# Weight casts moved into the first block's loads, and transfers to disjoint parts no longer ordered, in a hybrid decoder layer

## The chip, the cores and the metric

One Trainium2 chip, all 8 cores. Each core runs the same program on one element of the batch. The metric is the device time of the slowest core in microseconds (us), as a median over runs. Some executions of the kernels here fell into a slower state (the cores of a die at a lower mean clock, and a time 2 to 15% longer).

## The reference, cut to what matters

```python
# x: (8, 4096, 1024) float32, one sequence per core
z = h @ w_in                         # -> q | k | v | ssm_u | gates
y_attn = dilated attention, 3 groups of 4 heads, mixed by their softmax denominators
y_ssm  = GLU(gelu(s5_ssm(u)))        # 32 groups of 16 channels, 64 complex states each
mix = (sig(g_s) * (y_ssm @ w_ssm_proj) + sig(g_a) * (y_attn @ w_attn_proj)) @ w_out
h = layer_norm(ALPHA * h + mix)
ff = square(relu(h @ w_up)) @ w_down # 1024 -> 4096 -> 1024
h = layer_norm(ALPHA * h + ff)
```

## The kernel before

The program is written as operations with declared reads and writes of *resources*. A list scheduler fixes the order on each engine ahead of time; semaphores enforce what the resources imply. A transfer must wait, on the queue that issues it, for the last writer of every resource it writes to have *landed*:

```python
for w in writes:
    if w.w is not None and (dma or w.w.dma or w.w.eng != eng or eng != "pe"):
        dep(w.w)                       # write after write, whatever part was written
    ...
```

The stages: U projection and preparation of the SSM matrices; then six attention rounds (two head pairs by three dilations) beside 32 SSM groups, called the mixer stage here; then eight channel blocks of 512 tokens (gates, output projection, up, down). The parts the change touches:

```python
# preparation, per batch of two groups: three stores into disjoint parts, one resource
sres = [sw_res.res[g0 + j] for j in range(GB)]
dma("sp", dst[:, :, 0:640], st.ap, [st], sres)
dma("sp", dst[64:128, :, 640:896], st.ap[0:64, :, 384:640], [st], sres)
dma("sp", dst[0:64, :, 640:896], st.ap[64:128, :, 384:640], [st], sres)
# Toeplitz part: one buffer used twice
for off in range(2):
    for t in range(8): ...             # matmuls, then a copy into mst
    dma("sp", sw_d[:, :, 896 + off*128 : 1024 + off*128]..., mst.ap..., [mst], [mw_res])
# SSM group: two halves in, two halves out
for hf in range(2):
    dma("sp", ug.ap[:, hf, :], ..., [u_res.res[ft]], [ug])
for t in range(2):
    dma("act", y_d[g, :, t*8 : t*8+8]..., ysg.ap[:, t, :], [ysg], [y_res.res[g]])
# weights to bf16: 50 half pieces, memory to memory, paced by the projection's copies
wcast.append(lambda pace, c=c_: dma("pool", dst[i, c], src[i, c]..., pace, [...]))
for name in ("glu", "gate", "sp", "ap", "out", "up", "dn"): ...
# channel blocks: a ring of eight 8 KB slots, filled from the bf16 copies
dma("sp", slot.ap[:, 0:sz], dst[i], res.res[2*i : 2*i+2], [slot])
```

The softmax here doesn't subtract the row's maximum and nothing guards it: scores larger than these inputs give would overflow.

Of the kernel before, what the change touches and what calls it, by code (L numbers as in the profile page):

```python
# [362 lines left out]
def build_program():  # L363
# [33 lines left out]
    tabs_d = dram_tmp("tab_scratch", [32, 128, 2, 256], F32)  # L397
    sw_d = dram_tmp("sw_scratch", [32, 128, 1152], BF16)
    wb = {}
# [4 lines left out]
    u_res = Buf(None, 4)  # L404
    y_res = Buf(None, 32)
    ya_res = Buf(None, 16)
    tabs_res = Buf(None, 16)
    sw_res = Buf(None, 32)
    mw_res = Buf(None, 1)
# [248 lines left out]
    bigAs, bigBs = [f4(), f4()], [f4(), f4()]  # L658
    stg = [ar.alloc([GB, 640], BF16) for _ in range(3)]
    ar.seek(T2, c32.span[0])  # L660
    WSfs = [f4(), f4()]
    stg += [ar.alloc([GB, 640], BF16) for _ in range(2)]
    obi = 0
# [19 lines left out]
    for gb in range(NBATCH):  # L683
        g0 = gb * GB
        st, WSf = stg[gb % len(stg)], WSfs[gb % 2]
        (wA, wB), (lA, lB) = outer_pair(gb)
        tt("dve", WSf.ap, wA.ap, wB.ap, ALU.subtract, [wA, wB], [WSf])
        tt("dve", st.ap[:, :, 384:640], lA.ap.rearrange(flat), lB.ap.rearrange(flat), ALU.subtract, [lA, lB], [st])
        bk = banks[6 + gb % 2]
        for g in range(GB):  # L690
            for hf in range(2):
                lhs = WSf.ap[:, g, hf * 8:hf * 8 + 8, :].rearrange("p s h -> p (s h)")
                tr(bk.ap[:, (g * 2 + hf) * 128:(g * 2 + hf + 1) * 128], lhs, ident_f, [WSf, smP], [bk])
                mm(cols[hf].ap[:, (g0 + g) * 16:(g0 + g + 1) * 16], lhs, c1.ap[:, g0 + g, :], True, True,
                   [WSf, c1], [cols[hf]])
        wx = st.ap[:, :, 0:384].rearrange("p g (f q) -> p g f q", f=2)
        src = bk.ap.rearrange("p (g f q) -> p g f q", g=GB, f=2)
        cp("act", wx[:, :, :, 0:128], src, [bk], [st])
        cp("act", wx[:, :, :, 128:192], src[:, :, :, 0:64], [bk], [st])
        sres = [sw_res.res[g0 + j] for j in range(GB)]  # L700
        dst = sw_d[g0:g0 + GB].rearrange("g p q -> p g q")
        dma("sp", dst[:, :, 0:640], st.ap, [st], sres)
        dma("sp", dst[64:128, :, 640:896], st.ap[0:64, :, 384:640], [st], sres)
        dma("sp", dst[0:64, :, 640:896], st.ap[64:128, :, 384:640], [st], sres)
    ar.seek(argm.span[0], Xb.span[0])
    colb = [ar.alloc([512], BF16) for _ in range(2)]
    ar.seek(Q1u, A0)
    mst = ar.alloc([32, 8, 16], BF16)
    cp("act", colb[0].ap, cols[0].ap, [cols[0]], [colb[0]])
    tt("dve", colb[1].ap, cols[1].ap, sb_("ddiag"), ALU.add, [cols[1], smB], [colb[1]])  # L710
    n = 0
    for off in range(2):
        for t in range(8):
            bk = banks[4 + n % 4]
            n += 1
            d = 128 + 16 * (7 - t)
            mm(bk.ap, shf.ap[:, d:d + 128], colb[1 - off].ap, True, off == 0, [shf, colb[1 - off]], [bk])
            if off:
                d = 128 - 16 * (t + 1)
                mm(bk.ap, shf.ap[:, d:d + 128], colb[1].ap, False, True, [shf, colb[1]], [bk])  # L720
            cp("act" if t % 2 else "dve", mst.ap[:, :, t, :], bk.ap.rearrange("p (g h) -> p g h", h=16), [bk], [mst])
        dma("sp", sw_d[:, :, 896 + off * 128:1024 + off * 128].rearrange("g p q -> p g q"),
            mst.ap.rearrange("p g t h -> p g (t h)"), [mst], [mw_res])

# [37 lines left out]
    tabb = [ar.alloc([2, 256], F32) for _ in range(NS)]  # L762
    swb = [ar.alloc([1152], BF16) for _ in range(NS)]
    ugb = [ar.alloc([2, 256], BF16) for _ in range(NS)]
    t12 = ar.alloc([2, 256], F32)
# [6 lines left out]
    def ssm_in(g):  # L772
        tb, sw, ug = tabb[g % NS], swb[g % NS], ugb[g % NS]
        ft, h0 = g // 8, (g % 8) * 16
        for hf in range(2):
            dma("sp", ug.ap[:, hf, :], u_d[ft, h0:h0 + 16, hf * 8:hf * 8 + 8].rearrange("h s c -> s h c"),
                [u_res.res[ft]], [ug])
        dma("sp", sw.ap, sw_d[g], [sw_res.res[g], mw_res], [sw])
        dma("sp", tb.ap, tabs_d[g], [tabs_res.res[g // 2]], [tb])

    def ssm_z(g):
        sw, ug, bk = swb[g % NS], ugb[g % NS], banks[6]
        for z in range(2):
            for hf in range(2):
                o = hf * 192 + z * 64
                mm(bk.ap[:, z * 256:(z + 1) * 256], sw.ap[:, o:o + 128], ug.ap[:, hf, :], hf == 0, hf == 1,
                   [sw, ug], [bk], skip_group_check=True)

# [9 lines left out]
    def ssm_y(g):  # L798
# [11 lines left out]
        for t in range(2):  # L810
            dma("act", y_d[g, :, t * 8:t * 8 + 8].rearrange("h t c -> t h c"), ysg.ap[:, t, :], [ysg], [y_res.res[g]])

# [30 lines left out]

    for name in ("glu", "gate", "sp", "ap", "out", "up", "dn"):
        for i in range(len(wb[name][2].res) // 2):
# [169 lines left out]
    y2T = ar.alloc([4, 512], BF16, nres=4)  # L1015
    yab = ar.alloc([2, 512], BF16)
    sg = ar.alloc([512], F32)
    gsb, gab = ar.alloc([512], F32), ar.alloc([512], F32)
    ar.seek(E0, S1)
    yf = ar.alloc([4, 512], F32)  # L1020
    mixin = ar.alloc([8, 512], BF16, nres=8)
# [30 lines left out]
    def last_use(slot):  # L1052
        rs = slot.res[0]
        return max([o.seq for o in rs.r.values()] + [rs.w.seq if rs.w is not None else 0])

    def load_piece(name, i):
        slot = min((r for r in ring if id(r) not in live), key=last_use)
        live.add(id(slot))
        dst, _, res, sz = wb[name]
        dma("sp", slot.ap[:, 0:sz], dst[i], res.res[2 * i:2 * i + 2], [slot])  # L1060
        return slot
# [27 lines left out]
    def load_g(blk):  # L1089
        P.at("p3l", 6)  # L1090
        dma("pool", xTb.ap, xB_d[blk], [], [xTb])
        for kc in range(4):
            src = y_d[kc * 8:(kc + 1) * 8].rearrange("g h t c -> (g h) t c")[:, 2 * blk:2 * blk + 2, :]
            dma("sp", yf.ap[:, kc, :].rearrange("p (t c) -> p t c", t=2), src, [y_res.res[kc * 8 + j] for j in range(8)], [yf])
        act(yT.ap, yf.ap, AF.Gelu_apprx_tanh, [yf], [yT])
        for p4 in range(2):
            dma("sp", yab.ap[:, p4, :].rearrange("p (r c) -> p r c", r=2), ya_d[p4, :, 2 * blk:2 * blk + 2, :],
                [ya_res.res[p4 * 8 + blk]], [yab])

# [72 lines left out]
    def stage_up(blk):  # L1172
        P.at("p3", 7)
        for up in range(8):
            piece = load_piece("up", up)
            for m4 in range(4):
# [31 lines left out]
    for blk in range(NB):  # L1208
# [6 lines left out]
        P.at("p3", 7)  # L1215
        pcs = [load_piece("dn", q) for q in range(4)]
        if nxt:
            wo = [load_piece("out", oh) for oh in range(2)]
        pcs2 = [load_piece("dn", 4 + q) for q in range(2)]
        for t in range(TB):  # L1220
# [5 lines left out]
        if nxt:  # L1226
            done(*wo)
        pcs2 += [load_piece("dn", 6 + q) for q in range(2)]
        for t in range(TB):
# [73 lines left out]
```

## Time and profile before

| | before |
|---|---|
| median of 4 runs | 2152.30 us (2149.72 to 2153.1) |
| profiled run, slowest core | 2179.7 us |
| first load of the GLU weights, mean of the 8 cores | 694 us |
| from there to the last output store of block 1, mean of the 8 cores | 470.7 us |

The first GLU load ("first glu load") can only be issued when the last projection has read the input, so it marks how long the token mixers take. The second span (its end is the eighth store of the output) covers channel blocks 0 and 1, and so the place to which the change moves the casts. The lines of this profile stand in the prediction.

### The profile page before, as it was taken

Reading aid. Unit: us, or ns where it says so; the run is one execution under the profiler, and the core shown is the slowest. Engines: PE = TensorE matmul, PEld = TensorE weight load, DVE = VectorE, ACT = ScalarE, POOL = GpSimd, SP = SyncE. Lnnn points to the kernel's source line nnn. Section 1 sums busy time; section 2 is a strip of 40 time slices with the busy share of each in tenths; the row PEclk is TensorE's granted clock in tenths of the full one; section 3 lists DMA queues with packets and bytes.
Section 4 is the critical chain, followed back from the end, with each engine's and each line's share of the span. In section 5 each row is a group of like instructions: output and inputs, shape, how many; then the busy total and the mean of one; then the engine's idle time right before and its main releaser. Section 6 shows DMA issues by size and latency. Waiting matters only on the chain.

```text
span 2179.7 us, 31231 instructions; the slowest of 8 cores (2140.6 to 2179.7 us)
## 1 busy us (share of the span) xinstructions
PE 1929.6 (89%) x10468; PEld 943.1 (43%) x10468; DVE 952.5 (44%) x1396; ACT 696.2 (32%) x1053; POOL 300.2 (14%) x338
## 2 busy tenths in 40 slices
PE   3898278866879769999999999999999999999996
PEld 1455144634445334444444444444444444444443
DVE  6641255523432443364255355355345436424523
ACT  2553244533335623313312422421421421321120
POOL 6651012211210200100100100010010010010000
PEclk8999589978889889999999999999999999988898
DMA  9867567876763754456466466357447445533430
GB/s 167 175 197 113 117 156 155 151 140 145 153 133 128 233 168 152 150 172 243 140 192 241 136 188 251 136 158 276 142 144 250 181 140 186 216 107 136 176 116 39
DMA packets 112380, 359.71 MB, mean 165 GB/s; under 512 B 18240, under 2 KB 55488, under 8 KB 85184
## 3 DMA queue, kind: packets, MB, share of 16 engines
q1 hardware_dynamic: 79344, 265.33, 35.9%
q0 software_dynamic: 24176, 83.99, 19.5%
q10 hardware_dynamic: 8704, 8.39, 1.2%
q8 instruction: 88, 1.44, 0.3%
q14 instruction: 68, 0.56, 0.1%
HBM read 356.72 MB, written 74.97 MB: 198 GB/s over the span
## 4 chain that ended last, share of the span: by engine, by line
PE 66%; DMA 16%; DVE 6%; ACT 5%; issue 4%; ACTq 1%; SPq 1%; POOL 1%; DVEq 0%; POOLq 0%
PE ps L450 65%; DMA sw_scratch<-arena 6%; DMA y_scratch<-arena 5%; DVE arena L490 4%; ACT arena L496 2%; DMA arena<-u_scratch 2%; ACT arena L462 2%; DVE arena L480 1%; PE ps L455 1%; ACTq L440 1%; SPq L440 1%; ACT L462 1%; DMA arena<-x_tile 1%; DVE arena L1075 1%; DMA tab_scratch<-arena 0%
## 5 line engine op out<-in xcount | busy, mean ns | idle before, releaser
L450 PE MATMUL ps<-arena 128*128 128x512 bf16 (+3 forms) x10148 | 1912.1, 352 | 194.7 <-ACT arena L496 62.6
L450 PEld LDWEIGHTS ps<-arena 128*128 128x128 bf16 (+1 forms) x10148 | 926.8, 105 | 1162.2 <-issue 408.7
L462 ACT ACTIVATE arena<-ps 128x512 f32<-128x512 f32 (+2 forms) x384 | 261.0, 680 | 434.6 <-PE ps L450 340.8
L480 DVE TENSOR_TENSOR arena<-arena 128x512 f32<-128x512 f32 (+7 forms) x267 | 187.5, 725 | 232.2 <-ACT arena L462 165.3
L490 DVE SCALAR_TENSOR_TENSOR arena<-ps,arena 128x512 bf16<-128x512 f32 x256 | 176.9, 691 | 253.1 <-ACT arena L462 253.1
L480 POOL TENSOR_TENSOR arena<-arena 128x512 bf16<-128x512 f32 (+1 forms) x128 | 161.8, 1267 | 802.7 <-DVE arena L480 696.0
L480 DVE TENSOR_TENSOR arena<-ps,arena 128x512 f32<-128x512 f32 (+1 forms) x193 | 127.6, 688 | 328.7 <-PE ps L450 269.6
L462 ACT ACTIVATE arena<-arena 128x512 f32<-128x512 f32 (+6 forms) x186 | 101.3, 547 | 319.1 <-DVE arena L1077 262.0
L496 ACT CAST arena<-ps 128x512 bf16<-128x512 f32 (+1 forms) x217 | 120.8, 569 | 215.5 <-PE ps L450 138.4
L490 DVE SCALAR_TENSOR_TENSOR arena<-arena,ps 128x512 f32<-128x512 f32 x128 | 87.1, 686 | 216.6 <-PE ps L450 215.1
L490 DVE SCALAR_TENSOR_TENSOR arena<-arena 128x1024 f32<-128x1024 f32 (+1 forms) x131 | 167.1, 1276 | 21.7 <-ACT arena L462 6.6
L462 ACT ACTIVATE arena<-ps,arena 128x512 f32<-128x512 f32 x128 | 86.0, 686 | 177.7 <-POOL arena L480 140.7
L440 POOL DMA_DIRECT2D out<-arena x32 | 17.3, 542 | 646.6 <-DVE arena L490 646.6
L1075 DVE BATCH_NORM_STATS2 arena<-arena 128x6 f32<-128x512 f32 x128 | 88.8, 694 | 12.9 <-DVE arena L1075 0.5
L462 ACT ACT_TABLE_LOAD x42 | 53.9, 1283 | 121.0 <-DVE arena L1077 106.0
L496 ACT COPY arena<-ps 128x512 f32<-128x512 f32 (+1 forms) x64 | 51.1, 799 | 97.7 <-DMA y_scratch<-arena 56.8
L455 PE MATMUL ps<-arena 128*128 128x128 bf16 (+1 forms) x320 | 40.9, 248 | 38.8 <-ACT arena L496 22.2
L496 ACT CAST arena<-arena 128x1024 bf16<-128x1024 f32 x32 | 33.4, 1045 | 104.3 <-DVE arena L490 104.3
L455 PEld LDWEIGHTS ps<-arena 128*128 128x128 bf16 (+1 forms) x320 | 30.5, 126 | 57.3 <-issue 56.6
L480 DVE TENSOR_TENSOR arena<-arena,ps 128x512 f32<-128x512 f32 x64 | 41.0, 682 | 6.5 <-PE ps L450 6.3
L486 POOL TENSOR_SCALAR arena<-arena 128x256 f32<-128x256 f32 x32 | 39.9, 1248 | 15.6 <-DMA tab_scratch<-arena 13.0
L497 DVE CAST arena<-ps 128x512 bf16<-128x512 f32 x8 | 5.5, 692 | 71.0 <-DMA sw_scratch<-arena 61.0
(28 smaller groups left out, 166.2 us busy)
## 6 DMA issues: line engine op xcount, KB each, us to landing
arena<-wb_up SPq DMA_DIRECT2D x64, 1024.0 KB, 10.6
arena<-wb_dn SPq DMA_DIRECT2D x64, 1024.0 KB, 5.9
arena<-wb_gate SPq DMA_DIRECT2D x32, 1024.0 KB, 5.9
arena<-wb_out SPq DMA_DIRECT2D x16, 1024.0 KB, 4.9
arena<-x POOLq DMA_DIRECT2D x32, 512.0 KB, 9.2
out<-arena POOLq DMA_DIRECT2D x32, 512.0 KB, 4.0
arena<-sw_scratch SPq DMA_DIRECT2D x32, 288.0 KB, 7.1
arena<-x_tile POOLq DMA_DIRECT2D x8, 1024.0 KB, 49.4
```

The lines of the kernel that those rows point to most:

```text
L440: return P.add(eng, lambda e: e.dma_start(out=out, in_=in_), R(*reads), R(*writes), dma=True, nbytes=nb)
L450: return P.add("pe", lambda e: e.matmul(out, lhsT, rhs, start=start, stop=stop, **kw), R(*reads), R(*writes), cost=c)
L455: return P.add("pe", lambda e: e.transpose(out, in_, ident), R(*reads), R(*writes), cost=c)
L462: return P.add("act", lambda e: e.activation(out, in_, func, bias=bias, scale=scale), R(*reads), R(*writes), cost=c, aset=ASETS.get(func))
L480: return P.add(eng, lambda e: e.tensor_tensor(out, in0, in1, op), R(*reads), R(*writes), cost=ew_cost(eng, out, [in0, in1], True))
L486: return P.add(eng, lambda e: e.tensor_scalar(out, in0, s1, None, op0), R(*reads), R(*writes), cost=c)
L490: return P.add("dve", lambda e: e.scalar_tensor_tensor(out, in0, scalar, in1, op0, op1), R(*reads), R(*writes), cost=160.0 + 1.06 * fsize( ...
L496: return P.add("act", lambda e: e.copy(out, in_), R(*reads), R(*writes), cost=c)
L497: return P.add(eng, lambda e: e.tensor_copy(out, in_), R(*reads), R(*writes), cost=c)
L1075: P.add("dve", (lambda hf_: lambda e: e.bn_stats(st6[:, hf_ * 6:hf_ * 6 + 6], xb.ap[:, hf_ * 512:hf_ * 512 + 512]))(hf), R(xb), R(m), cost ...
```

## The change

The intent is twofold. Transfers that write disjoint parts get a resource each, so that none waits for a sibling to land; the two stores of the Toeplitz matrix become one with long rows. And the up and down weights are no longer cast from memory to memory during the mixer stage: the loads of the first channel block cast them into the ring, and the slot is stored from there for the other seven blocks. The diff, cut to its core:

```diff
-    y_res = Buf(None, 32)
+    y_res = Buf(None, 64)
-    sw_res = Buf(None, 32)
+    sw_res = Buf(None, 96)
...
-        dma("sp", dst[:, :, 0:640], st.ap, [st], sres)
-        dma("sp", dst[64:128, :, 640:896], st.ap[0:64, :, 384:640], [st], sres)
-        dma("sp", dst[0:64, :, 640:896], st.ap[64:128, :, 384:640], [st], sres)
+        dma("sp", dst[64:128, :, 640:896], st.ap[0:64, :, 384:640], [st.res[1]], sres[1])
+        dma("sp", dst[0:64, :, 640:896], st.ap[64:128, :, 384:640], [st.res[1]], sres[2])
+        dma("sp", dst[:, :, 0:640], st.ap, [st], sres[0])
...
-    ar.seek(Q1u, A0)
-    mst = ar.alloc([32, 8, 16], BF16)
+    ar.seek(Q1, A0)
+    mst = ar.alloc([32, 2, 8, 16], BF16, nres=16)
...
-        dma("sp", sw_d[:, :, 896 + off * 128:1024 + off * 128].rearrange("g p q -> p g q"),
-            mst.ap.rearrange("p g t h -> p g (t h)"), [mst], [mw_res])
+    dma("sp", mw_d, mst.ap.rearrange("p g o t h -> p g (o t h)"), [mst], [mw_res])
...
-                [u_res.res[ft]], [ug])
-        dma("sp", sw.ap, sw_d[g], [sw_res.res[g], mw_res], [sw])
+                [u_res.res[ft]], [ug.res[hf]])
+        dma("sp", sw.ap[:, 0:896], sw_d[g], sw_res.res[3 * g:3 * g + 3], [sw.res[0]])
+        dma("sp", sw.ap[:, 896:1152], mw_d[:, g, :], [mw_res], [sw.res[1]])
...
-            dma("act", y_d[...], ysg.ap[:, t, :], [ysg], [y_res.res[g]])
+            dma("act", y_d[...], ysg.ap[:, t, :], [ysg], [y_res.res[g * 2 + t]])
...
-    for name in ("glu", "gate", "sp", "ap", "out", "up", "dn"):
+    for name in ("glu", "gate", "sp", "ap", "out"):
...
+        if first:
+            was = P.stream, P.prio
+            P.at("p3c", 5)
+            dma("pool", slot.ap[:, 0:sz], src[i].rearrange("p k c -> p (k c)"), [], [slot])
+            dma("sp", dst[i], slot.ap[:, 0:sz], [slot], res.res[2 * i:2 * i + 2])
+            P.at(*was)
+        else:
+            dma("sp", slot.ap[:, 0:sz], dst[i], res.res[2 * i:2 * i + 2], [slot])
...
-            piece = load_piece("up", up)
+            piece = load_piece("up", up, blk == 0)
...
-        pcs = [load_piece("dn", q) for q in range(4)]
+        pcs = [load_piece("dn", q, blk == 0) for q in range(4)]
```

The cuts are the new scratch tables, the choice of a ring slot, the same step for the staging buffers, for the gelu input and the attention input of the channel blocks (one resource a part), and the other down loads.

More of the change, by code (lines that the diff above doesn't have):

```diff
@@ L397, in build_program @@
     tabs_d = dram_tmp("tab_scratch", [32, 128, 2, 256], F32)
-    sw_d = dram_tmp("sw_scratch", [32, 128, 1152], BF16)
+    sw_d = dram_tmp("sw_scratch", [32, 128, 896], BF16)
+    mw_d = dram_tmp("mw_scratch", [128, 32, 256], BF16)
     wb = {}
@@ L658, in build_program @@
     bigAs, bigBs = [f4(), f4()], [f4(), f4()]
-    stg = [ar.alloc([GB, 640], BF16) for _ in range(3)]
+    stg = [ar.alloc([GB, 640], BF16, nres=2) for _ in range(3)]
     ar.seek(T2, c32.span[0])
     WSfs = [f4(), f4()]
-    stg += [ar.alloc([GB, 640], BF16) for _ in range(2)]
+    stg += [ar.alloc([GB, 640], BF16, nres=2) for _ in range(2)]
     obi = 0
@@ L687, in build_program @@
         tt("dve", WSf.ap, wA.ap, wB.ap, ALU.subtract, [wA, wB], [WSf])
-        tt("dve", st.ap[:, :, 384:640], lA.ap.rearrange(flat), lB.ap.rearrange(flat), ALU.subtract, [lA, lB], [st])
+        tt("dve", st.ap[:, :, 384:640], lA.ap.rearrange(flat), lB.ap.rearrange(flat), ALU.subtract, [lA, lB], [st.res[1]])
         bk = banks[6 + gb % 2]
@@ L697, in build_program @@
         src = bk.ap.rearrange("p (g f q) -> p g f q", g=GB, f=2)
-        cp("act", wx[:, :, :, 0:128], src, [bk], [st])
-        cp("act", wx[:, :, :, 128:192], src[:, :, :, 0:64], [bk], [st])
-        sres = [sw_res.res[g0 + j] for j in range(GB)]
+        cp("act", wx[:, :, :, 0:128], src, [bk], [st.res[0]])
+        cp("act", wx[:, :, :, 128:192], src[:, :, :, 0:64], [bk], [st.res[0]])
+        sres = [[sw_res.res[(g0 + j) * 3 + part] for j in range(GB)] for part in range(3)]
         dst = sw_d[g0:g0 + GB].rearrange("g p q -> p g q")
-        dma("sp", dst[:, :, 0:640], st.ap, [st], sres)
-        dma("sp", dst[64:128, :, 640:896], st.ap[0:64, :, 384:640], [st], sres)
-        dma("sp", dst[0:64, :, 640:896], st.ap[64:128, :, 384:640], [st], sres)
+        dma("sp", dst[64:128, :, 640:896], st.ap[0:64, :, 384:640], [st.res[1]], sres[1])
+        dma("sp", dst[0:64, :, 640:896], st.ap[64:128, :, 384:640], [st.res[1]], sres[2])
+        dma("sp", dst[:, :, 0:640], st.ap, [st], sres[0])
     ar.seek(argm.span[0], Xb.span[0])
     colb = [ar.alloc([512], BF16) for _ in range(2)]
-    ar.seek(Q1u, A0)
-    mst = ar.alloc([32, 8, 16], BF16)
+    ar.seek(Q1, A0)
+    mst = ar.alloc([32, 2, 8, 16], BF16, nres=16)
     cp("act", colb[0].ap, cols[0].ap, [cols[0]], [colb[0]])
@@ L720, in build_program @@
                 mm(bk.ap, shf.ap[:, d:d + 128], colb[1].ap, False, True, [shf, colb[1]], [bk])
-            cp("act" if t % 2 else "dve", mst.ap[:, :, t, :], bk.ap.rearrange("p (g h) -> p g h", h=16), [bk], [mst])
-        dma("sp", sw_d[:, :, 896 + off * 128:1024 + off * 128].rearrange("g p q -> p g q"),
-            mst.ap.rearrange("p g t h -> p g (t h)"), [mst], [mw_res])
+            cp("act" if t % 2 else "dve", mst.ap[:, :, off, t, :], bk.ap.rearrange("p (g h) -> p g h", h=16), [bk],
+               [mst.res[off * 8 + t]])
+    dma("sp", mw_d, mst.ap.rearrange("p g o t h -> p g (o t h)"), [mst], [mw_res])
     P.at("tabs", 3)
@@ L762, in build_program @@
     tabb = [ar.alloc([2, 256], F32) for _ in range(NS)]
-    swb = [ar.alloc([1152], BF16) for _ in range(NS)]
-    ugb = [ar.alloc([2, 256], BF16) for _ in range(NS)]
+    swb = [ar.alloc([1152], BF16, nres=2) for _ in range(NS)]
+    ugb = [ar.alloc([2, 256], BF16, nres=2) for _ in range(NS)]
     t12 = ar.alloc([2, 256], F32)
@@ L786, in ssm_z @@
                 mm(bk.ap[:, z * 256:(z + 1) * 256], sw.ap[:, o:o + 128], ug.ap[:, hf, :], hf == 0, hf == 1,
-                   [sw, ug], [bk], skip_group_check=True)
+                   [sw.res[0], ug.res[hf]], [bk], skip_group_check=True)
     def ssm_scan(g):
@@ L810, in ssm_y @@
         for t in range(2):
-            dma("act", y_d[g, :, t * 8:t * 8 + 8].rearrange("h t c -> t h c"), ysg.ap[:, t, :], [ysg], [y_res.res[g]])
+            dma("act", y_d[g, :, t * 8:t * 8 + 8].rearrange("h t c -> t h c"), ysg.ap[:, t, :], [ysg], [y_res.res[g * 2 + t]])
     for g in range(NS):
@@ L1015, in build_program @@
     y2T = ar.alloc([4, 512], BF16, nres=4)
-    yab = ar.alloc([2, 512], BF16)
+    yab = ar.alloc([2, 512], BF16, nres=2)
     sg = ar.alloc([512], F32)
@@ L1019, in build_program @@
     ar.seek(E0, S1)
-    yf = ar.alloc([4, 512], F32)
+    yf = ar.alloc([4, 512], F32, nres=4)
     mixin = ar.alloc([8, 512], BF16, nres=8)
@@ L1053, in last_use, with load_piece @@
         rs = slot.res[0]
-        return max([o.seq for o in rs.r.values()] + [rs.w.seq if rs.w is not None else 0])
-    def load_piece(name, i):
+        return max([o.seq for o in list(rs.r.values()) + rs.rd] + [rs.w.seq if rs.w is not None else 0])
+    def load_piece(name, i, first=False):
         slot = min((r for r in ring if id(r) not in live), key=last_use)
         live.add(id(slot))
-        dst, _, res, sz = wb[name]
-        dma("sp", slot.ap[:, 0:sz], dst[i], res.res[2 * i:2 * i + 2], [slot])
+        dst, src, res, sz = wb[name]
+        if first:
[6 more added lines that the diff above has]
+            dma("sp", slot.ap[:, 0:sz], dst[i], res.res[2 * i:2 * i + 2], [slot])
         return slot
@@ L1093, in load_g @@
             src = y_d[kc * 8:(kc + 1) * 8].rearrange("g h t c -> (g h) t c")[:, 2 * blk:2 * blk + 2, :]
-            dma("sp", yf.ap[:, kc, :].rearrange("p (t c) -> p t c", t=2), src, [y_res.res[kc * 8 + j] for j in range(8)], [yf])
+            dma("sp", yf.ap[:, kc, :].rearrange("p (t c) -> p t c", t=2), src,
+                [y_res.res[(kc * 8 + j) * 2 + blk // 4] for j in range(8)], [yf.res[kc]])
         act(yT.ap, yf.ap, AF.Gelu_apprx_tanh, [yf], [yT])
@@ L1097, in load_g @@
             dma("sp", yab.ap[:, p4, :].rearrange("p (r c) -> p r c", r=2), ya_d[p4, :, 2 * blk:2 * blk + 2, :],
-                [ya_res.res[p4 * 8 + blk]], [yab])
+                [ya_res.res[p4 * 8 + blk]], [yab.res[p4]])
     def stage_g(blk):
@@ L1215, in build_program @@
         P.at("p3", 7)
-        pcs = [load_piece("dn", q) for q in range(4)]
+        pcs = [load_piece("dn", q, blk == 0) for q in range(4)]
         if nxt:
             wo = [load_piece("out", oh) for oh in range(2)]
-        pcs2 = [load_piece("dn", 4 + q) for q in range(2)]
+        pcs2 = [load_piece("dn", 4 + q, blk == 0) for q in range(2)]
         for t in range(TB):
@@ L1227, in build_program @@
             done(*wo)
-        pcs2 += [load_piece("dn", 6 + q) for q in range(2)]
+        pcs2 += [load_piece("dn", 6 + q, blk == 0) for q in range(2)]
         for t in range(TB):
```

## The prediction

> **What bounds the kernel now.** I read the page's slices first, then the windows table, the chain, the waits, and the transfer issues; all on the slowest core (span 2179.7 us). The slices show two programs in one: the token mixers (up to about 700 us) with TensorE (PE) full of holes, and the channel-block loop after about 810 us with PE full.
>
> ```profile
> PE   3898278866879769999999999999999999999996
> ...
> PEclk8999589978889889999999999999999999988898
> DMA  9867567876763754456466466357447445533430
> ```
>
> One digit is 54.5 us. From slice 16 on PE is at 9 everywhere. Slice 5 (218 to 272 us) is 2, and its clock is 5. The windows table (busy us, instructions, granted clock, DMA share, GB/s) puts sizes on it:
>
> ```profile
> 150.00:200.00 50.00, 50.00 (x450) 32.46 (x449) 16.46 (x22) 20.89 (x39) 12.49 (x16) 1.00 0.66 115
> 200.00:250.00 50.00, 12.17 (x103) 7.33 (x102) 0.89 (x2) 3.51 (x6) 2.02 (x4) 0.64 0.66 110
> ...
> 400.00:500.00 100.00, 68.04 (x560) 41.18 (x558) 39.44 (x62) 40.77 (x66) 17.47 (x22) 0.86 0.78 149
> 500.00:600.00 100.00, 73.89 (x602) 45.55 (x602) 39.19 (x59) 35.86 (x51) 18.28 (x23) 0.85 0.67 141
> ...
> 1000.00:1100.00 100.00, 100.00 (x465) 45.36 (x464) 35.09 (x54) 34.77 (x50) 11.21 (x10) 1.00 0.51 169
> ```
>
> No engine is busy in 200:250, and in 400:600 none is near full. So the first stage is bound by waits, not by an engine. Which waits, the chain of work that ended last tells, first in shares, then in order of time:
>
> ```profile
> PE ps L450 65%; DMA sw_scratch<-arena 6%; DMA y_scratch<-arena 5%; DVE arena L490 4%; ACT arena L496 2%; DMA arena<-u_scratch 2%; ACT arena L462 2%; DVE arena L480 1%; PE ps L455 1%; ACTq L440 1%; SPq L440 1%; ACT L462 1%; DMA arena<-x_tile 1%; DVE arena L1075 1%; DMA tab_scratch<-arena 0%
> ```
>
> ```profile
> 189.50 5.85 DMA sw_scratch<-arena
> 196.20 31.12 DMA sw_scratch<-arena
> 227.44 2.10 DMA sw_scratch<-arena
> 230.33 2.42 DMA sw_scratch<-arena
> 232.87 2.10 DMA sw_scratch<-arena
> ...
> 488.38 15.12 DMA y_scratch<-arena
> ```
>
> From 66 to 248 us the chain is one store into sw_scratch after another: each batch writes three disjoint parts, but all three carry the same resource, so the sync queue waits for one to land before it issues the next. The later pieces are the second half of each y store waiting for the first, on ScalarE's queue. The waits view says who pays:
>
> ```profile
> DVE arena L497 <- DMA sw_scratch<-arena: 61.0, 1, 61.0
> ACT arena L496 <- DMA y_scratch<-arena: 56.8, 12, 10.0
> PE ps L450 <- DVE arena L497: 38.4, 2, 37.8
> ...
> SPq L222 <- DMA arena<-u_scratch: 183.7, 30, 17.3
> SPq L222 <- DMA sw_scratch<-arena: 98.3, 27, 30.3
> ```
>
> The 61 us wait is the copy of the second half of the Toeplitz matrix (mst), whose buffer is held until the first half's store lands at 248.2. PE stands in that queue for 37.8 us. Attention's first round also needs the memory of the preparation, so its chain starts only at 257 us, and the state-space groups (SSM) at 262.
>
> [...] the shortest pieces above are 2.10 us for 64 KB, and in traffic they are 5 to 8, once 31. [...] clock 0.64 in 200:250, 0.85 in 400:600, 1.00 where PE is dense. A filled hole is thus worth more than its length.
>
> **The change, part by part.**
>
> 1. *Store order in the preparation.* 48 stores of 16 batches wait only for their data; before, 32 of them waited for a sibling to land too. Batches pass PE's f32 transposes at 46, 53, 56, 60, 65, 70 us, some 4.8 us each while the five staging buffers last, then at 78, 94, 111 ... 175: about 10.5 each, because buffers come free with landings. Unblocked, the last batch is due near 46 + 15 x 4.8 = 118 us, say 130 with the tables beside it. The two mst stores of 4096 packets of 256 B become one of 128 rows of 16 KB, and no copy waits for a store. But mst now lies on the U staging buffers, so it waits for the last u store (147.5, landed about 150). Its 24 matmuls and 16 copies took 180 to 188 and 248 to 254, so some 14 us: mst is ready at about 165, SSM starts near 172 to 180 instead of 262.
>
> 2. *What that start is worth on PE.* PE is full from 100 to 212 us anyway (U, first projections), so the 85 us of earlier start are not all gained. PE's busy time before 695 us, where the last projection ends and the first ring loads are issued, is 165 (to 212) + 1 (to 250) + 337 (250 to 695) = 503 us, so 192 us are idle: 47 before 100 us, where the x loads bind (DMA share about 1.0) and nothing changes; 38 in 212 to 250, which goes entirely; 108 in 250 to 695.
>
> 3. *u loads and y stores.* Of the chain, y_scratch is 5.2% (113 us) and u_scratch 1.9% (41 us). These waits disappear: the two halves no longer wait for each other, and ScalarE no longer holds the exponentials of attention behind a landing. In place of these 154 us stands the next limit, the order of work on PE, ScalarE and VectorE. An attention round costs PE about 41 us of projection + 20 of attention + 6 of SSM, and took 60 to 95. I take 60% of the 108 us as recoverable: 65. The clock should rise from 0.86 to about 0.9; of 337 us that is some 10.
>
> 4. *Weight casts leave the mixer stage.* 32 casts of up and down, 512 KB each, are no longer in GpSimd's queue among the SSM products (its waits for wb_up and wb_dn pacing were 86 + 65 + 23 us, mostly idle time that costs nothing) nor on the DMA engines: each cast is 16 packets of 32 KB, which averaged 3660 ns in the trace's transfer records, so 3.7 us of all 16 engines per cast, 117 us in all. I count this inside the 60%.
>
> 5. *They come back in channel block 0.* A piece is now a cast load of 1 MB plus a store of 1 MB, instead of a load of 1 MB. The x_blk load has exactly that form:
>
> ```profile
> arena<-wb_up SPq DMA_DIRECT2D x64, 1024.0 KB, 10.6
> ...
> arena<-x_blk POOLq DMA_DIRECT2D x8, 1024.0 KB, 13.5
> ```
>
> Its packets average 676 ns for 8 KB in the transfer records, 128 x 676 / 16 = 5.4 us of all engines; a plain load or store 128 x 340 / 16 = 2.7 us. So 8.1 instead of 2.7 us per piece, against 6.9 us of PE per piece (32 matmuls of 216 ns). Sixteen pieces add 16 x 5.4 = 86 us of transfers. From 695 to 811 us the DMA share was 0.76 and 0.60 (80 us of 116), from 811 to 984 it was 0.46 (80 of 173). Six up pieces fit in front, during the gates and the serial layer norms; ten come later. The shares then come to (80 + 6 x 5.4) / 116 = 0.97 and (80 + 10 x 5.4) / 173 = 0.77. It fits, but not without stalls: I allow 15 us.
>
> *Sum:* 38 + 65 + 10 - 15 = 98 us on this core. The seven other blocks (172.3 us each) stay. 2152 - 98 x 0.97 (I take a little off, as the timed runs are 1% shorter) gives **2057 us**.
>
> **The rivals.** *(a) Another wait takes over.* With the stores gone, the mixer stage could stay at its 75% PE: the fixed order of instructions, the single score banks and the exponential (1.02 us a unit, 96 units) give a latency chain of their own. For it: in 250 to 475 us, two and a bit rounds took 219 us although the y stores were only part of the chain. Then only the 38 us and about 25 more come back: 2152 - 63 + 15 = 2104. *(b) Block 0 starves.* The weight store sits in the sync queue and waits there for its cast load (13.5 us); glu, gate and down loads behind it wait too. If each of the 16 costs 4 us on PE, that is 64 instead of 15 us lost: 2107. Against it: eight ring slots and the slack of the layer norms. *(c) Fuller recovery.* If attention and SSM become PE-bound, all 108 us of holes go and the clock reaches 0.95: 38 + 108 + 25 - 10 = 161, so 1993. Against it: from 600 to 650 us, when the y stores thin out, PE was busy for 36 of 50 us only. [...] Some cores show clock 0.81 for stretches of 200 us[...].
>
> **Range and chances.** (a) and (b) each near 2105, (c) near 1995; both (a) and (b) at once would give about 2155. So 2020 to 2105. The 2% line is 2109: faster 0.90, within 2% 0.08, slower 0.02.
>
> **What would show it.** Right: the chain after has no run of sw_scratch stores and y_scratch well under 1%; PE above 0.8 in every slice from 2 to 12; the first SSM loads at 165 to 185; the first glu load at 585 to 615 instead of 695; the time from the first to the third glu load, which holds block 0 (696 to 993 us before, 297), 5 to 30 us longer; later blocks at 172. Wrong: the first glu load after 640 (rival a), block 0 more than 40 us longer with PE idle under DMA names (rival b), or a first glu load before 570 (rival c).

## The result, and the profile after

The change takes 2053.36 us (median of 4 runs, of which one, 2177.2 us, is slow), against 2152.3 for the kernel before: a ratio of 0.954 (95% interval 0.952 to 0.956). A ratio is always the mean time of one kernel's fast runs over that of the other's fast runs of the same rounds, so not quite the ratio of the medians. The predicted time was 2057.

The slices of the page (one digit is 51.3 us here) and the chain's shares, slowest core, answer to those of before:

```profile
PE   3898777999977697999999999999999999999996
...
PEclk8999987999988898999999999999999999999998
DMA  9946887551169949974565447366356543633521
...
PE ps L451 72%; DVE arena L491 4%; ACT arena L497 3%; ACT arena L463 2%; DVE arena L481 2%; DMA arena<-wb_out 1%; DMA y_scratch<-arena 1%; ACTq L441 1%; PE ps L456 1%; DMA wb_out<-w_out 1%; DMA arena<-x_tile 1%; ACT L463 1%; DVE arena L1084 1%; DMA tab_scratch<-arena 1%; DMA wb_ap<-w_attn_proj 0%
```

The 2 in PE's slice 5 is gone (the first slice is 1, as in the prediction), sw_scratch is out of the chain, and y_scratch fell from 5% to 1%. But PE is not full from slice 2 on: 7 stands in slices 5 to 7, where the transfer engines are at 8, 8 and 7, and PE dips again in slices 12 to 14 (564 to 718 us, 6 in the last) and 16 (770 to 821 us). The windows of the mixer stage (busy us by engine PE, PEld, DVE, ACT, POOL; then granted clock, DMA share, GB/s):

```profile
200.00:250.00 50.00, 39.98 (x265) 21.48 (x264) 26.00 (x42) 23.10 (x32) 11.71 (x13) 0.95 0.86 179
...
300.00:350.00 50.00, 33.74 (x162) 16.27 (x160) 14.40 (x24) 11.19 (x19) 10.84 (x12) 0.77 0.81 184
...
400.00:500.00 100.00, 95.04 (x805) 56.89 (x804) 51.28 (x76) 53.84 (x81) 16.45 (x15) 1.00 0.42 110
```

Where PE is at 95% the DMA share is 0.42; where it is at 67 to 80% it is above 0.8. The chain in order of time has, among its long pieces:

```profile
254.16 24.57 DMA y_scratch<-arena
...
299.25 9.19 DMA wb_ap<-w_attn_proj
...
318.31 7.75 DMA wb_out<-w_out
...
333.46 11.77 DMA wb_out<-w_out
...
795.27 29.59 DMA arena<-wb_out
```

The first four lie in 254 to 346 us, among the 18 casts that are left (glu, gate, sp, ap, out; issued from 197 to 347 us). The last lies in channel block 0: an output weight load that took 29.6 us to land, among cast loads. In numbers, over the eight cores: the first glu load comes at 568 us instead of 694 (126 us gained), and from there to the end of block 1 it takes 492.6 us instead of 470.7 (21.9 lost). The difference, 104 us, is the 99 of the times but for the difference between profiled and timed runs.

So the predicted total came out, with a larger gain and a larger loss than in its sum (113 and 15). Whether it came out for the stated reasons is another matter, and what the experiments are for.

### The profile page after: what moved, and what is told of

Same layout as the page of the kernel before. It is cut to its first block, busy times and chain, and to the rows that moved or that the text cites.

```text
span 2052.5 us, 31367 instructions; the slowest of 8 cores (2035.6 to 2052.5 us)
## 1 busy us (share of the span) xinstructions
PE 1876.9 (91%) x10468; PEld 924.2 (45%) x10468; DVE 957.9 (47%) x1396; ACT 695.1 (34%) x1053; POOL 295.2 (14%) x322
## 4 chain that ended last, share of the span: by engine, by line
PE 73%; DVE 8%; DMA 6%; issue 6%; ACT 5%; ACTq 1%; POOL 1%; DVEq 0%; POOLq 0%; SPq 0%
PE ps L451 72%; DVE arena L491 4%; ACT arena L497 3%; ACT arena L463 2%; DVE arena L481 2%; DMA arena<-wb_out 1%; DMA y_scratch<-arena 1%; ACTq L441 1%; PE ps L456 1%; DMA wb_out<-w_out 1%; DMA arena<-x_tile 1%; ACT L463 1%; DVE arena L1084 1%; DMA tab_scratch<-arena 1%; DMA wb_ap<-w_attn_proj 0%
## 5 line engine op out<-in xcount | busy, mean ns | idle before, releaser
L451 PE MATMUL ps<-arena 128*128 128x512 bf16 (+4 forms) x10148 | 1859.2, 345 | 118.2 <-DMA arena<-x_tile 27.4
L451 PEld LDWEIGHTS ps<-arena 128*128 128x128 bf16 (+2 forms) x10148 | 909.3, 104 | 1049.1 <-issue 215.0
L481 DVE TENSOR_TENSOR arena<-arena 128x512 f32<-128x512 f32 (+7 forms) x267 | 193.7, 750 | 180.0 <-ACT arena L463 167.1
L1084 DVE BATCH_NORM_STATS2 arena<-arena 128x6 f32<-128x512 f32 x128 | 88.8, 694 | 12.2
L456 PEld LDWEIGHTS ps<-arena 128*128 128x128 bf16 (+1 forms) x320 | 28.9, 121 | 61.7 <-issue 61.5
L488 DVE TENSOR_SCALAR arena<-arena 128x512 f32<-128x512 f32 (+2 forms) x19 | 9.5, 503 | 42.8 <-POOL arena L487 42.4
```

Of the source, the lines that this page charges most:

```text
L451: return P.add("pe", lambda e: e.matmul(out, lhsT, rhs, start=start, stop=stop, **kw), R(*reads), R(*writes), cost=c)
L456: return P.add("pe", lambda e: e.transpose(out, in_, ident), R(*reads), R(*writes), cost=c)
L481: return P.add(eng, lambda e: e.tensor_tensor(out, in0, in1, op), R(*reads), R(*writes), cost=ew_cost(eng, out, [in0, in1], True))
L488: return P.add(eng, lambda e: e.tensor_scalar(out, in0, s1, s2, op0, op1), R(*reads), R(*writes), cost=c)
L1084: P.add("dve", (lambda hf_: lambda e: e.bn_stats(st6[:, hf_ * 6:hf_ * 6 + 6], xb.ap[:, hf_ * 512:hf_ * 512 + 512]))(hf), R(xb), R(m), cost ...
```

## The experiments

Two theories at the start. **Theory 1**, the prediction's: the order of the transfers makes the gain, and the moved casts are a net loss in block 0. **Theory 2**: the casts, while they run beside attention and SSM, are dear, and moving them out is a good part of the gain. Results are summed up here; the column "scaled" is the ratio times 2152 and makes runs on different chips comparable within the intervals (some 4 us either way for the change, up to 29 for uy_back). "Front" is the first glu load and "blocks 0, 1" the span from it to the last output store of block 1, both means over the eight cores of the profiled run.

| kernel | median us | ratio to before (95%) | scaled | front | blocks 0, 1 |
|---|---|---|---|---|---|
| before | 2152.3 | 1 | 2152 | 694 | 470.7 |
| the change | 2053.4 | 0.954 (0.952 to 0.956) | 2053 | 568 | 492.6 |
| order_only | 2106.2 | 0.975 (0.971 to 0.978) | 2097 | 640 | 471.8 |
| weights_only | 2095.9 | 0.968 (0.966 to 0.971) | 2084 | 605 | 492.4 |
| prep_back | 2084.4 | 0.963 (0.960 to 0.966) | 2072 | 596 | 493.2 |
| uy_back | 2093.9 | 0.962 (0.948 to 0.975) | 2070 | 587 | 492.2 |
| order_pad | 2095.3 | 0.972 (0.964 to 0.980) | 2092 | 623 | 472.1 |
| tiny_casts | 2078.3 | 0.953 (0.948 to 0.959) | 2052 | 576 | 493.4 |
| after_pad | 2054.4 | 0.951 (0.948 to 0.955) | 2047 | 569 | 491.9 |
| order_nohold | 2098.0 | 0.972 (0.966 to 0.979) | 2093 | 631 | 477.1 |
| late_store | 2034.8 | 0.942 (0.939 to 0.945) | 2027 | 567 | 475.9 |
| all_first | 2031.9 | 0.940 (0.937 to 0.944) | 2024 | 530 | 512.4 |
| late_r4 | 2005.5 | 0.930 (0.924 to 0.937) | 2002 | 538 | 477.6 |
| ordered_r4 | 2040.7 | 0.946 (0.942 to 0.950) | 2036 | 567 | 480.7 |

A median here is over all runs, slow ones too (uy_back and tiny_casts had two each; the change, weights_only, prep_back and order_pad one each). All twelve gave correct results. The scheduler plans every kernel anew. The lists of PE, VectorE and ScalarE are in the same order in order_only, order_pad, order_nohold and tiny_casts, and in the change and after_pad; every other comparison has a changed order of instructions in it too.

### The two halves apart: order_only and weights_only

order_only is the change with the weight part undone:

```diff
-    for name in ("glu", "gate", "sp", "ap", "out"):
+    for name in ("glu", "gate", "sp", "ap", "out", "up", "dn"):
-            piece = load_piece("up", up, blk == 0)
+            piece = load_piece("up", up)
     # and the same for every load of "dn"
```

> Only the unordered transfers; up and down weights are cast memory to memory in the mixer stage, as before. Theory 1 (the order of transfers makes the gain, the weight move costs block 0 some 27 us and gives little back): first glu load at 570 to 590 us, first to third glu load back near 298 us, time 2025 to 2045. Theory 2 (the weight move frees the mixer stage and is a good part of the gain): first glu load at 630 or later, time over 2085.

weights_only is the kernel before with that part alone:

```diff
-    for name in ("glu", "gate", "sp", "ap", "out", "up", "dn"):
+    for name in ("glu", "gate", "sp", "ap", "out"):
+    load_piece(name, i, first=False)   # as in the change; up and dn with first = (blk == 0)
```

> Only the weight move; all transfers ordered as before. Theory 1: first glu load near 690, first to third glu load 320 to 330, time 2160 to 2180, so slower than before. Theory 2: first glu load near 640, time about 2110 to 2130.

Theory 1 missed on both. Order alone brought 55 us (scaled) where it was to bring 107 to 127, and the weight move alone, which was to make the kernel slower, brought 68. Theory 2 was right on order_only and too small on weights_only (640 us of front and 2110 to 2130 expected, 605 and 2096 measured). Block 0 loses its 21 us in both kernels that move the casts and in neither that does not; but the front gains 89 us by the weight move alone (694 to 605), and 72 with the order already changed (640 to 568). The order is worth 54 us of front without the weight move and 37 with it. So the two share a cause, and the larger part is the weight move.

What the casts do stands in order_only's chain, in order of time:

```profile
298.44 9.86 DMA wb_ap<-w_attn_proj
...
319.04 8.76 DMA wb_out<-w_out
...
411.60 41.31 DMA ya_scratch<-arena
...
471.52 45.10 DMA arena<-bias_t
```

ya_scratch is a store of 128 KB, bias_t a load of 256 KB. In the kernel before, their medians to landing were 5.0 and 8.3 us; here two of them took 41 and 45, and attention stood behind each. The windows of the same kernel show PE and the engines' load:

```profile
400.00:450.00 50.00, 33.11 (x172) 15.86 (x172) 14.25 (x23) 19.43 (x32) 9.93 (x13) 0.88 0.93 147
450.00:500.00 50.00, 37.25 (x385) 26.57 (x385) 17.08 (x25) 14.62 (x25) 10.45 (x14) 0.91 0.86 142
500.00:550.00 50.00, 26.94 (x157) 13.08 (x158) 15.32 (x23) 16.84 (x24) 5.17 (x7) 0.70 0.74 144
```

PE has 27 to 37 of 50 us where the change has 95 of 100. That compares two orders of instructions; tiny_casts, below, keeps the order.

### The order, part by part: prep_back and uy_back

prep_back is the change with the preparation's stores ordered as before (one resource per staging buffer and group, two mst stores through one buffer; an SSM group then loads both parts in one transfer again, which the cut leaves out):

```diff
-        dma("sp", dst[64:128, :, 640:896], ..., [st.res[1]], sres[1])
-        dma("sp", dst[0:64, :, 640:896], ..., [st.res[1]], sres[2])
-        dma("sp", dst[:, :, 0:640], st.ap, [st], sres[0])
+        dma("sp", dst[:, :, 0:640], st.ap, [st], sres)
+        dma("sp", dst[64:128, :, 640:896], ..., [st], sres)
+        dma("sp", dst[0:64, :, 640:896], ..., [st], sres)
```

> The change with the preparation's stores ordered as before (one resource per staging buffer and group, two mst stores through one buffer). Theory 1: the hole after 212 us returns, time 2053 + 38 to 60 = 2091 to 2113. Rival (the SSM and attention stage makes up for a late start, since y stores no longer hold it): no more than 2070.

uy_back is the change with the two halves of a u load and of a y store ordered again:

```diff
-                [u_res.res[ft]], [ug.res[hf]])
+                [u_res.res[ft]], [ug])
-            dma("act", ..., [ysg], [y_res.res[g * 2 + t]])
+            dma("act", ..., [ysg], [y_res.res[g]])
```

> The change with the two halves of each u load and of each y store ordered again. Theory 1: about 65 us of holes return, time 2053 + 50 to 80 = 2103 to 2133. Rival (a landing wait of 5 us per group is hidden by prefetch and by other work): no more than 2075.

Undoing the preparation's part costs 19 us scaled (28 of front, 31 in the medians), less than the 38 to 60 of theory 1 and a little more than its rival allowed. The hole did return (the last Toeplitz store was issued at 252 to 257 us, before at 251 to 262), but part of it was made up later. Undoing u and y costs some 16 (19 of front; the fast runs were 2070, 2077 and 2094, so the interval is wide), not 50 to 80. In that respect the rival was right: with the up and down casts gone, a landing wait per group is mostly hidden. The two parts add up to 47 us of front, against 37 for the whole order (605 to 568), so each is known to about 10 us only.

### What a cast costs beside attention: tiny_casts, order_pad, order_nohold

Three ways in which a cast could hurt: its bytes on the transfer engines; its wait in GpSimd's fixed order, among the SSM products; and its packets, 32 KB each. tiny_casts is the change plus 32 casts of 16 rows of 128 B in the old places, told to the scheduler as full-sized, so that the order of the mixer stage is that of order_only (PE's and ScalarE's lists of instructions are the same but for line numbers):

```diff
+    o = dma("pool", dmy_d[j], src[i, h0:h0 + 16, 0, 0:64], pace, [])
+    o.nbytes = 64 * 4096 * 2           # what the scheduler reckons with
```

> The change, plus 32 tiny cast transfers (16 rows of 128 B) in the places of the up and down casts, with the same waits on GpSimd and the same hold on their pacing buffers; the order of the mixer stage's instructions is that of order_only. Theories A and bytes: first glu load near 565 to 580, time near the change's 2053, at most 2065. Theory of GpSimd's waits or of the order of instructions: first glu load near 646, time 2125 to 2135 (block 0's loss on top).

The front is 576 us against 640 in order_only. So 64 of the 72 us go with the bytes; the waits on GpSimd and the order of instructions account for the other 8 at most (one die of this run had a lower clock, 0.944 against 0.962, and the later fronts; the other die alone has 573, against 638 in order_only). The stretch in which order_only had 27 to 37 of 50 us of PE is full, with the same instructions in the same order:

```profile
400.00:450.00 50.00, 48.65 (x476) 33.15 (x473) 26.18 (x39) 25.96 (x44) 15.23 (x20) 1.00 0.53 141
450.00:500.00 50.00, 49.73 (x430) 29.41 (x429) 24.23 (x38) 28.74 (x40) 10.31 (x16) 1.00 0.32 78
500.00:550.00 50.00, 47.47 (x371) 25.60 (x369) 22.63 (x37) 28.33 (x39) 3.26 (x7) 0.97 0.15 27
```

order_pad is order_only with the rows of the bf16 copies padded, in the same order of instructions:

```diff
-        wb[name] = (dram_tmp("wb_" + name, [n, 128, sz], BF16), ...)
+        wb[name] = (dram_tmp("wb_" + name, [n, 128, sz + 64], BF16)[:, :, 0:sz], ...)
```

> As order_only (same order of instructions on PE, VectorE, ScalarE and the sync queue), but the rows of the bf16 weight copies in memory are padded by 128 B, so that a cast moves 64 packets of 8 KB and not 16 of 32 KB; the bytes stay. Theory A (the 32 KB packets hold each transfer engine for some 4 us, and small transfers queue behind one of them at every packet): first glu load near 570 to 600 instead of 646, time 2050 to 2075, and the 41 and 45 us landings of ya_scratch and bias_t are gone. Theory B (bytes on the engines, or GpSimd's paced waits, are what costs): 2095 to 2110 as before.

The packets became 8 KB as meant, but the front moved only from 640 to 623, and the time by less than the intervals. In the trace's transfer records a moment of order_only shows the crowding itself: while 12 to 16 engines were at work on a 32 KB packet, most 2 us steps started 10 to 70 other packets; in the steps from 450 to 456 us, with none running, 425 to 464. In the trace of the kernel before, from 200 to 700 us, a step with 12 to 16 engines on such a packet started 36 others on average, a step with none 249. With 8 KB packets the engines are as full, and y_scratch and bias_t still stand in the chain with up to 30 us. Packet size is a part, some 17 of 72 us, not the cause.

order_nohold is order_only without the wait of the compute engines for a paced cast to land before they write the buffer that paced it:

```diff
+                if id(d) in self.casts and not op.dma:
+                    continue           # the cast never reads that buffer
```

> As order_only, in the same order of instructions, but the compute engines do not wait for a paced cast to land before they write its pacing buffer again two rounds later (the cast never reads that buffer, so there is no race). In order_only's chain these waits (wb_ap, wb_out, wb_up) were 36 us. If they were true cost: first glu load at 605 to 620 instead of 646, time 2070 to 2085. If the transfers' load on the engines is the cost and these waits only stand in front of others: first glu load at 630 or later, time 2090 to 2105.

The front moved by 9 us (640 to 631, with 618 to 642 on single cores), the time by nothing clear. (Its 477.1 for blocks 0 and 1 comes from cores 0 and 1, at a lower clock in this run; the others have 470 to 475.) So the waits on wb_ap and wb_out in the chain stand mostly in front of other waits: in its chain y_scratch pieces of 13 to 24 us stand in that stretch instead. By elimination and by tiny_casts, what costs is the casts' load on the engines while SSM and attention pass small pieces through memory. How the remaining 45 or so us split between the engines' time and the memory's was not tried.

### The casts that are left, and block 0: after_pad, late_store, all_first, late_r4

after_pad is the change with the padding of order_pad.

> The change with the same padding, for the 18 casts that are left in the mixer stage; same order of instructions. Theory A: the 24.6 us y landing at 254 us and the waits on wb_ap and wb_out shrink, first glu load at 545 to 560, time 2030 to 2042. Theory B: within 5 us of the change.

Nothing (569 against 568 us of front). That was, after order_pad, the second miss of the view that packet size is the cost.

late_store issues the store of a fresh piece when the piece has been used, not when it lands:

```diff
-            dma("sp", dst[i], slot.ap[:, 0:sz], [slot], res.res[2 * i:2 * i + 2])
+            late[id(slot)] = (dst[i], slot.ap[:, 0:sz], slot, res.res[2 * i:2 * i + 2])
     def done(*slots):
         for r in slots:
+            if id(r) in late:
+                o_, i_, s_, w_ = late.pop(id(r))
+                dma("sp", o_, i_, [s_], w_)
```

> The change with the store of a freshly cast weight piece issued when the piece has been used, not when it lands, so that loads of output weights do not stand behind it on the sync queue. If the sync queue's waits make block 0's extra 27 us: first to third glu load 300 to 310 us, time 2028 to 2040. If the transfers themselves are too slow (casts and stores fill the engines) or GpSimd issues the down casts too late: 318 to 330 us, time 2045 to 2060.

Blocks 0 and 1 take 475.9 us, 17 less than in the change and 5 more than before, inside what was expected if the sync queue's waits were the cause. In the change's trace that queue had indeed waited for casts, on SP:

```profile
SPq L222 <- DMA arena<-w_down: 88.1, 7, 37.5
...
SPq L222 <- DMA arena<-w_up: 22.6, 4, 9.4
```

and PE had waited twice, 17 us in all:

```profile
809.31 6.44 PE L451 MATMUL ps<-arena 128*128 128x512 bf16 x16 [7.72 <-DMA arena<-w_down]
825.10 12.08 PE L451 MATMUL ps<-arena 128*128 128x512 bf16 x47 [9.34 <-DMA arena<-wb_out]
```

But the queue's waits did not make these two. The second output weight load was issued at 795 us, when PE gave its slot free, 5 us after the store ahead of it had gone; in late_store it is issued as late, 220 us after the first glu load in both (mean of the cores). What differs is what was on the engines by then. In the change the first four down casts came in a bunch, behind products that stand ahead of them in GpSimd's order of instructions, the first of which had waited for VectorE:

```profile
764.35 1.27 POOL L481 TENSOR_TENSOR arena<-arena 128x512 bf16<-128x512 f32 x1 [89.54 <-DVE arena L481]
...
771.05 1.62 POOL L441 DMA_DIRECT2D arena<-w_down  x3
...
776.68 0.57 POOL L441 DMA_DIRECT2D arena<-w_down  x1 [1.57 <-PE ps L451]
```

The fourth took 32.5 us to land (27 to 33 on the eight cores), and the output load 29.6. In late_store the scheduler put the first two ahead of those products: the first came 177 us after the first glu load, not 196 (means of the cores), the fourth landed in 8 to 11 us, and the stores went out behind the output loads. So the late store brings 17 of the 22 us, as far as the traces tell through a lighter load on the transfer engines at that moment; how much of it comes from the later stores and how much from the earlier casts was not tried.

all_first is late_store with every weight cast by its first load, none in the mixer stage (`load_piece("glu", 0, blk == 0)` and so on).

> late_store, with every weight piece of the first block cast by its first load, none in the mixer stage. First glu load (a cast load now) at 530 to 550; but the first gates start with eight cast loads of 5.4 us each on the engines, 43 us where eight plain loads took some 22, so 20 to 30 us are lost there: time 2015 to 2045.

Front 530, but blocks 0 and 1 take 512 us: the first gates wait for their cast loads, and what the mixers gain over late_store (37 us) goes there. It is the change's own trade, overdone.

late_r4 is late_store with the 18 casts paced in rounds 4 and 5, and without the hold of order_nohold:

```diff
-                if rnd > 0 and t % 2 == 1 and wcast:
+                if rnd > 3 and t % 2 == 1 and wcast:
```

> late_store, with the 18 casts that are left paced in rounds 4 and 5, when the SSM groups are done and the transfer share of the change's trace was 0.17 to 0.27, and without the hold on the pacing buffer. If a cast costs because it loads the engines while SSM and attention need small transfers: the holes at 250 to 350 us fill, first glu load at 535 to 555, time 2005 to 2025. If those holes have another cause: first glu load at 560 or later, time 2030 or more.

2005.5 us, the fastest of all: 48 us under the change and 147 under the kernel before. Its windows:

```profile
200.00:250.00 50.00, 47.89 (x385) 27.90 (x383) 31.48 (x48) 26.61 (x38) 10.10 (x9) 1.00 0.55 150
250.00:300.00 50.00, 49.32 (x460) 32.35 (x459) 30.65 (x50) 26.51 (x39) 10.68 (x9) 1.00 0.53 143
300.00:350.00 50.00, 48.39 (x492) 34.51 (x491) 33.68 (x52) 30.44 (x49) 11.46 (x9) 1.00 0.59 163
```

PE has 48 of 50 us at clock 1.00 in the stretch where the change has 34 to 41 at 0.77 to 0.95. all_first has no casts there either and shows the same 47, 49, 48. (late_r4 has two edits at once, and the scheduler chose another order for both kernels, the same one in this stretch. So for these 18 casts load and order are not told apart; for the other 32, tiny_casts did it.) The 18 casts, now issued from 425 to 509 us, after the last SSM group and beside projections that load little but their weights, cost little: the front is 8 us behind that of all_first.

### Is the order worth anything without the casts: ordered_r4

ordered_r4 is late_r4 with all transfers ordered as before (weights_only plus the edits of late_store and late_r4).

> late_r4 (2005 us) with all transfers ordered as in the kernel before: how much the order is worth once no weight cast runs beside SSM. If the order costs by itself (each wait is a landing, and the preparation's stores are a serial chain whatever else runs): the hole after 212 us stays, first glu load near 580 to 595 instead of 540, time 2040 to 2060. If the order was dear only because the casts made landings long: first glu load under 560, time under 2025. If the two do not interact: 2005 + 52 (order_only against before) = 2057.

2040.7 us, 35 more than late_r4, and the front at 567 instead of 538, between what the first two readings expected (580 to 595, and under 560). So the order has a price of its own, of some 30 us, even without weight casts beside SSM. Its first attention round loads its bias at 202 to 205 us; in late_r4 that is 138 to 140. The preparation stays a serial chain of landings without them. The 55 us that order_only gained are thus, as an estimate across two pairs of kernels, some 30 of the order itself, and the rest came from long landings that casts had made.

The run shows one thing more. The hole after 212 us, on which the prediction built its first 38 us, was for the most part not the order's. With the same order of transfers and of instructions up to there, but no weight casts, PE is busy for 37.5 us of this stretch instead of 12.2 (weights_only, with the order and the glu and gate casts, has 11.5):

```profile
200.00:250.00 50.00, 37.50 (x398) 26.89 (x397) 26.58 (x35) 22.05 (x31) 5.33 (x5) 0.83 0.57 150
```

The last Toeplitz store is issued at 214 to 217 us, in the kernel before at 251 to 262. The store of 31.12 us in the prediction's chain ran there from 196 to 227 us, beside eight glu and gate casts that were issued from 181 to 209 and landed by 226.

## Why the prediction was right, and where it was not

The number was right, the mechanism half so. That the total came within 4 us is in part luck: a gain 13 us larger than in the sum and a loss 7 us larger offset each other.

**Step 1, the store order in the preparation.** Its mechanism held. The last batch was predicted for 118 to 130 us; the last sw_scratch store was issued at 123 to 124 on every core. The mst store came at 182 to 183, not 165, because the u stores whose buffer it takes over came at 162 to 166 instead of 147.

**Steps 2 and 3, what the waits are worth.** These were mis-sized. "38 in 212 to 250, which goes entirely" and "65" for the u and y waits with the rest of the recoverable holes, were put down to the order. Undone one at a time, the preparation's part is worth 19 to 31 us and the u and y part some 16 to 19. The 38 us were read off the right store, but it was slow beside the glu and gate casts: ordered_r4 keeps the order and has a third of the hole. Nor is a share of the chain a price: in ordered_r4 y_scratch still has 4.2% of it (some 86 us, in pieces of mostly 4 to 8 us), and the whole order is worth 29 us of front there. The chain names the transfer that was waited for, not what made it slow. That a filled hole is worth more than its length shows right behind the one after 212 us: the eight 128x512 products at 249 us took 3.57 us, 446 ns each, at a granted clock of 0.50, and from 1000 to 1100 us 465 of them took 100 us, 215 ns each, at 1.00.

**Step 4, the weight casts leave the mixer stage.** This is the step that failed: "I count this inside the 60%", "mostly idle time that costs nothing". The casts' 117 us of engine time were worked out rightly (their 32 KB packets took 3660 ns on average, 3500 in the median) and then given no price of their own. Their going moved the front by 72 us (order_only to the change), 89 without the order. Since the 60% had been set from the holes as a whole, the sum came out at 113 of front against 126 measured: the holes were counted, their owner was in large part wrong.

**Step 5, block 0.** Right in kind, 22 us where 15 were allowed, inside the stated 5 to 30. PE's two waits in it were for transfers that landed late among casts and stores, as the sum of transfers had it; issuing the stores late brought 17 of the 22 back. Rival (b) named the store on the sync queue, which did wait, but the load that PE missed was not held by it. (Two slips in the sums change little: the records give a plain 8 KB packet 368 ns on average, with a median of 309, not 340, and an 8 KB packet of a cast load in the change 746, with a median of 625; and (c)'s 161 us make 1996 with the factor of 0.97, not 1993.)

**The signs.** Of those named in advance, the run of sw_scratch stores is gone, blocks from the third on take 172 us, and block 0 is within its bounds. PE is not above 0.8 in every slice from 2 to 12 (7 in four of them); y_scratch is at 1.2% of the chain and not well under 1%, in one piece of 24.6 us; the first SSM loads came at 126 to 127 us, but the first load of the Toeplitz part only at 189 to 191, where 165 to 185 was given; the first glu load came at 563 to 575 us, before the 585 to 615 that was given and on most cores before the 570 that was to be the sign of rival (c). Rival (a), another wait in place of the one removed, is what the change still had in 200 to 350 us; rival (c) is what late_r4 came near.

## What to carry to other kernels

A long wait for a small transfer has two questions in it: why is it waited for, and why did it take so long; when a 128 KB store takes 25 to 41 us instead of 5, look for what else is on the transfer engines in that stretch before cutting the dependency. Bulk traffic that nobody waits for is not free (with the bytes of 32 casts gone, the front came 64 us earlier here): put it beside the stage that passes little through memory, not where it happens to have issue slots. When a load is followed by a store of what it brought, issue the store when the piece has been used; here that brought 17 of the 22 us that block 0 had lost. And when a run hits its expected number, look in its trace for the wait that was said to go.
